# Two-block decoder step: other row ratios around the convolution norm, and means of the raw products one channel tile earlier

## The chip, the cores and the metric

The kernel runs on one core of a Trainium2 chip. The metric is the device time of one execution in microseconds. Three executions of the kernel before gave 1777.66 to 1778.84 us, with a median of 1777.99 us. A fourth one was profiled; the trace that is read here is of that one.

## What is computed

The reference has two blocks in a row on 256 tokens of 1024 channels. In the first, each of two layers normalises the tokens, shifts and scales them by rows that come from a conditioning vector, projects them, runs four branches (retention, short convolution, conformer convolution with a layer norm, attention), and merges them. Layer 0 does so for 256 context tokens too, so it works on 512 columns; layer 1 works on 256. A final norm ends the block. Cut to what matters:

```
for l in range(DEPTH):                                   # first block
    shift, scale, gate = split(silu(c) @ w_mod[l] + b_mod[l])
    h = rmsnorm(x, norm_w[l]) * (1 + scale) + shift
    p = split(h @ w_in[l])
    f = silu(layer_norm(dwconv31(glu(p.cf)) + b)) * silu(p.cf_z)   # "conv" branch
    merged = sum(sigmoid(g[i]) * (branch[i] @ w_branch[i]) for i in range(4))
    x = x + gate * (merged @ w_out[l])
x = rmsnorm(x, final_norm_w)
for i in range(2):                                       # second block
    m = split(silu(c_2) @ ada_w[i] + ada_b[i], 6)
    x = x + m.gt_m * rmsnorm(mixer_i(rmsnorm(x) * (1 + m.sc_m) + m.sh_m))
    x = x + m.gt_f * rmsnorm(conv_ffn(rmsnorm(x) * (1 + m.sc_f) + m.sh_f))
```

## The kernel before

**Products.** The channels lie on the 128 partitions in eight tiles (k = 0 to 7), the tokens on the free axis. Every product of a large weight is made of three: each 128x1024 chunk of a weight comes by DMA into `wr` (SyncE's queue), ScalarE rounds it to `wh` (L166), and VectorE subtracts, `wl` = `wr` - `wh` (L169); data are split into `r` pairs in the same way. TensorE then runs high by high, high by low and low by high (L189). Four `wh`/`wl` pairs exist, so ScalarE can round a chunk only when TensorE has let go of the one four chunks ago. In stages of 512 columns the results go through banks `pm`, of which there are four.

**Work beside the products.** Branch work is written as generators in a queue `hiq` (attention, the convolution's taps, `layer_norm`, `retention`). `pump(us)` (L192), called after each product, runs pieces of them against a credit; `until(st, key)` (L207) runs them to a mark: "att" is the end of attention, "ln" that of the convolution's norm.

**Modulation rows.** Shift, scale and gate of layer 1 and of the second block are matrix-vector products that VectorE makes, one weight row of 128x1024 at a time: a multiplication with a running sum whose full output goes to a scratch tile, so it is called `junk` in the trace (L498). The row is fetched on GpSimd's queue into one of two buffers `ad` (`fetch_row`, L483); the fetch of row n+2 is issued when row n has been used. A `wmodT` row is used twice in layer 0's part (two vectors, `sb_c` and `sb_c_ctx`), each of the 96 `adaT` rows once. There are 152 such instructions. They wait in a second queue `loq`; `pump` takes from it once its count `pumps`, which starts below zero, is above zero: `spare` grows by `ratio * us` and each row costs 1.15 of it (2.3 if used twice). `flush_lo` (L214) issues the rest before a place that needs the results: before layer 0's and layer 1's output product.

**Norms between the stages.** The first product after an output product is begun on raw data ("raw-product step", `start4`, L338): eight channel tiles times four outputs, and the norm's factors are multiplied in afterwards. A callback `mid(k)` is called within tile k: there the squares are summed by TensorE (`means` L549, or `row_sum` L407), `rsqrt` (L429; a ScalarE square root with a table load and a VectorE reciprocal) is taken, and `spread` (L441) copies a column to all 128 columns by a transpose (L443). ScalarE then brings the result out of the bank, and the next `r` pairs (`mod_tile` L558 in layer 1, `maker` L1466 in the second block) need it.

**Order.** A scheduler places each engine's instructions in one fixed list; an engine works its list in order, and what waits holds up what stands behind it.

Of the kernel before, what the change touches and what calls it, by code (L numbers as in the profile page):

```python
# [18 lines left out]
P = 128  # L19
# [85 lines left out]
class Core:  # L105
# [645 lines left out]
    def first_block(self):  # L751
        nc, A, cst = self.nc, self.A, self.cst
        with self.tc.manual_schedule():
            xs, ps, hs = self.start()
        self.last = self.end
        for l in range(2):
            N = 512 if l == 0 else 256
            if l == 1:
                rb = self.T()

                def mid(k):
                    if k == 4:
                        st["pc"] = self.psa()
                        self.means(st["pc"], 0, acc[0].groups(), True, True)
                    if k == 5:
                        st["r"] = self.small(4)
                        self.rsqrt(st["r"], st["pc"][:, 0:4])
                    if k == 7:
                        pb = self.psa()
                        for t in range(4):  # L770
                            self.spread(pb[:, t * P:(t + 1) * P], st["r"][:, t:t + 1])
                        self.act(rb, pb)
                ps, _ = self.start4(lambda k: raws[k], S + 2, mid=mid)
                hs = [(self.R(), self.R()) for _ in range(KT)]
            mod = lambda k, s: self.mod_tile(k, xs[k], rb, self.acol, self.mod[1], hs[k], s)
            norm = lambda p: self.normed(self.T(S), p, rb[:, :S])
            merged = self.mixer(l, hs, N, ps, mod, norm)
            del hs
            acc, st = [Sum(self) for _ in range(1 + l)], {}
            if l == 0:  # L780
                self.src.extend(self.quad(A["win"][1], 32, 36))
                self.flush_lo(lambda: self.done_mods[1])
                a1, sh = self.acol[:, :, 0], self.mod[1][:, 0:8, 0]
            else:
                self.src.extend(self.quad(A["rgi"], 8, 10))
                self.flush_lo(lambda: self.done_mods[2])
                self.ada_columns()
                a1, sh = self.afw, self.ada4[:, 0, 0]
            sh = self.shift_parts(sh, f"sh{l}")
            raws = []  # L790
            first = self.two_tiles(merged, N)
            for n in range(KT):
                ps = first[n] if n < 2 else self.tile_gemm(merged, N)
                for s in range(N // S):
                    c = slice(s * S, (s + 1) * S)
                    x = xs[n][:, c]
                    self.stt(x, ps[:, c], self.gate[l][:, n, s:s + 1], x, ALU.mult, ALU.add)
                q = self.T(N)
                self.act(q, xs[n][:, :N], AF.Square)
                acc[0].push(q)  # L800
                if n == KT - 1 and l == 0:
                    acc[0].push(None)
                if l == 1:
                    q = self.T(S)
                    self.act(q, xs[n][:, :S], AF.Square, scale=self.par("final_norm_w", n))
                    acc[1].push(q)
                raws.append(self.raw_tile(xs[n][:, :S], a1[:, n:n + 1], sh, n))
                self.pump(0.5)
        st = {}

        def mid(k):

            if k == 4:
                rows = self.psa()[0:2, :S]
                parts = [a.groups() for a in acc]
                for m in range(4):
                    self.row_sum(rows, m % 2, 2, [parts[m % 2][m // 2]], 1024, m == 0, m == 3)
                st["sb"] = self.row_copy(rows, 2, S)
            if k == 5:
                pc = self.row_columns(st["sb"], 2, S)  # L820
                r, s, t = [self.cst.tile([P, 2], F32, name="fin" + n) for n in "rst"]
                self.rsqrt(r, pc[:, :, 0])
                self.tt(t, r, r, ALU.mult)
                self.tt(t, t, pc[:, :, 1], ALU.mult)
                self.rsqrt(s, t)
                self.tt(s, s, r, ALU.mult)
                st["s"], st["r"], self.xx = s, r, t
        ps, _ = self.start4(lambda k: raws[k], S + 2, mid=mid)
        return [x[:, :S] for x in xs], ps, st["r"], st["s"]

# [51 lines left out]
    def mixer(self, l, hs, N, first, mod, norm):  # L882
        nc, A = self.nc, self.A
        NS = N // S
        bud = (3.0, 1.0)[l]
        self.pumps, self.spare = -(10, 30)[l], 0.0
        self.ratio = (0.5, 0.6)[l]
        if l:
            self.src.extend(self.mixer_chunks(l))
        self.ahead()  # L890
# [307 lines left out]

        gates(1, br[1], True, False)
        self.until(st, "att")  # L1200
        br[3] = []
        for i in range(4):
            z = silu2(proj())
# [85 lines left out]
            st["ret"] = 1  # L1289

        self.until(st, "ln")
        self.ratio = (0.6, 0.6)[l]
        self.hiq.append(retention())
        br[2] = []
        for i in range(4):
# [11 lines left out]
        return merged  # L1307


    def second_block(self, xs, ps, r, s):  # L1310
        nc, A, cst = self.nc, self.A, self.cst
        self.rgw = [self.load_plain(A["rgw"][g]) for g in range(4)]
        self.rgo = [self.load_plain(q) for q in self.quad(A["rgo"], 0, 2)]
        rb = self.psa()
        for i in range(2):
            self.spread(rb[:, S + i * P:S + (i + 1) * P], s[:, i:i + 1])
        for i in range(2):
            self.spread(rb[:, i * P:(i + 1) * P], r[:, i:i + 1])
        rs, rf = self.T1(), self.T1()
        self.act(rs, rb[:, S:])  # L1320
        self.act(rf, rb[:, :S])
        mk = self.maker(xs, rs, self.afw, self.ada4[:, 0, 0])
        first = lambda c: self.normed(self.T1(), ps[c], rs)

        def finish(k):

            self.stt(xs[k], xs[k], self.par("final_norm_w", k), rf, ALU.mult, ALU.mult)

        for i in range(2):
            nxt = self.quad(A["ffu"][i], 0, NFF)  # L1330
            mk = self.rglru(xs, mk, nxt, first, finish) if i == 0 else self.gla(i, xs, mk, nxt)
            nxt = self.quad(A["gli"], 0, 2) if i == 0 else ()
            mk = self.ffn(i, xs, mk, nxt)
# [505 lines left out]
def build(nc, tc, A):  # L1839
    with ExitStack() as ctx:  # L1840
        k = Core(nc, tc, ctx, A)
        with ExitStack() as c1:
            k.adp = c1.enter_context(tc.tile_pool(name="adp", bufs=2, reuse_waits="tile"))
            k.setup()
            k.t2 = c1.enter_context(tc.tile_pool(name="t2", bufs=58, reuse_waits="tile"))
            fin = k.first_block()
        k.t1 = ctx.enter_context(tc.tile_pool(name="t1", bufs=74, reuse_waits="tile"))
        k.g4 = ctx.enter_context(tc.tile_pool(name="g4", bufs=12, reuse_waits="tile"))
        k.second_block(*fin)

# [53 lines left out]
```

## Time and profile before

| | |
|---|---|
| median of three runs | 1777.99 us |
| the profiled execution | 1775.62 us |
| its span in the trace | 1773.8 us |
| TensorE busy | 1729.2 us, 97% of the span |
| VectorE busy | 1365.3 us, 77% |
| ScalarE busy | 915.8 us, 52% |
| `junk` on VectorE, 128 of one vector | 156.3 us, 51.1 us idle before them |
| clock of TensorE, mean of the span | 0.993 of full |

The page gives busy time and share of each engine first, then the span in 40 slices, the DMA queues, the chain that ended last, and the costliest groups of instructions with the idle time before them and its releaser. The timeline of an engine lists its instructions with start, duration and, in brackets, the idle time before with what ended it. A duration is longer than the distance to the next start where instructions overlap.

### The profile page before, as it was taken

To read this page: it belongs to the slowest core of one execution; us is meant where nothing else is said; L and a number is where in the kernel's file an instruction comes from. 1 tells how busy PE (TensorE), PEld (TensorE's weight loads), DVE (VectorE), ACT (ScalarE), POOL (GpSimd) and SP (SyncE) were. 2 spreads that over 40 slices of the span, in tenths; PEclk is the share of its full clock that TensorE was granted. 3 is DMA by queue.
4 is the path that set the end of the run, shared out by engine and by line. 5 is a ranking of instruction groups with operands and counts; after the bars stand their busy time and mean duration, and the time that the engine had idled before them with its cause. 6 is when DMAs were issued, how large, how long until landed. Compare 5 with 4: busy or idle time off the path is not lost.

```text
span 1773.8 us, 29675 instructions
## 1 busy us (share of the span) xinstructions
PE 1729.2 (97%) x11538; PEld 1552.3 (88%) x11538; DVE 1365.3 (77%) x2501; ACT 915.8 (52%) x1565; POOL 77.3 (4%) x161
## 2 busy tenths in 40 slices
PE   8999999899999999999999999999999999999998
PEld 5787788688978888898998999898999989989998
DVE  4797599976577786697499877779887669788864
ACT  5426642432342333546642554685776565656663
POOL 0000000011011110000000000100000000000000
PEclk9999999999999999999999999999999999999999
DMA  9433234467347674443376466632555633445553
GB/s 346 153 118 109 82 131 143 145 223 248 125 152 244 240 255 154 135 161 120 126 245 235 160 218 196 217 130 90 198 188 165 193 120 109 135 137 182 188 173 114
DMA packets 94302, 301.60 MB, mean 170 GB/s; under 512 B 10049, under 2 KB 11841, under 8 KB 94161
## 3 DMA queue, kind: packets, MB, share of 16 engines
q1 hardware_dynamic: 72096, 225.00, 37.9%
q0 software_dynamic: 19584, 71.31, 12.2%
q10 hardware_dynamic: 2480, 3.39, 0.6%
q8 instruction: 91, 1.49, 0.3%
q14 instruction: 51, 0.41, 0.1%
HBM read 298.61 MB, written 1.05 MB: 169 GB/s over the span
## 4 chain that ended last, share of the span: by engine, by line
PE 70%; issue 17%; DVE 6%; ACT 5%; DMA 1%; POOL 0%; DVEq 0%; POOLq 0%; ACTq 0%
PE pm L189 54%; PE pa L189 13%; ACT t L166 3%; DMA ad<-adaT 1%; DVE wl L169 1%; DVE t L169 1%; DVE t L186 1%; ACT wh L166 1%; PE pa L554 1%; PE pa L1129 1%; PE pa L1721 1%; PE pa L411 1%; DVE x L169 0%; PE pa L606 0%; ACT L166 0%
## 5 line engine op out<-in xcount | busy, mean ns | idle before, releaser
L189 PE MATMUL pm<-r,wh 128*128 128x256 f32 (+2 forms) x5344 | 1211.3, 320 | 16.0 <-ACT r L166 8.5
L189 PEld LDWEIGHTS pm<-r,wh 128*128 128x128 f32 x5344 | 889.7, 191 | 103.9 <-ACT r L166 12.8
L189 PE MATMUL pm<-r,wl 128*128 128x256 f32 (+2 forms) x2672 | 846.4, 319 | 0.5 <-DVE wl L169 0.5
L166 ACT ACTIVATE wh<-wr 128x1024 fp32r<-128x1024 f32 (+1 forms) x408 | 425.8, 1049 | 529.4 <-PE pm L189 395.7
L169 DVE TENSOR_TENSOR wl<-wr,wh 128x1024 fp32r<-128x1024 f32 (+1 forms) x408 | 492.2, 1210 | 174.7 <-ACT wh L166 165.4
L189 PEld LDWEIGHTS pm<-r,wl 128*128 128x128 f32 x2672 | 508.5, 191 | 35.9 <-issue 1.4
L498 DVE SCALAR_TENSOR_TENSOR junk<-ad,sb_c 128x1024 bf16<-128x1024 f32 x128 | 156.3, 1221 | 51.1 <-DMA ad<-adaT 41.0
L189 PE MATMUL pa<-r,wh 128*128 128x256 f32 (+1 forms) x864 | 168.7, 292 | 5.7 <-ACT r L166 5.4
L189 PEld LDWEIGHTS pa<-r,wh 128*128 128x128 f32 x864 | 137.6, 191 | 10.0 <-ACT r L166 6.0
L169 DVE TENSOR_TENSOR t<-t,t 128x256 f32<-128x256 f32 (+2 forms) x278 | 126.4, 470 | 17.5 <-ACT t L166 15.1
L186 DVE SCALAR_TENSOR_TENSOR t<-t,cfw,t 128x482 f32<-128x482 f32 (+29 forms) x240 | 130.7, 601 | 0.0
L189 PE MATMUL pa<-r,wl 128*128 128x256 f32 (+1 forms) x432 | 123.7, 291 | 0.0
L166 ACT ACTIVATE r<-t 128x256 fp32r<-128x256 f32 (+1 forms) x116 | 53.6, 470 | 93.8 <-DVE t L169 55.8
L166 ACT ACTIVATE t<-pm 128x256 f32<-128x256 f32 (+1 forms) x180 | 82.0, 456 | 21.6 <-PE pm L189 21.6
L189 PE MATMUL pa<-t,t 128*64 128x128 f32 (+3 forms) x668 | 89.5, 337 | 0.8 <-ACT t L166 0.8
L189 PEld LDWEIGHTS pa<-r,wl 128*128 128x128 f32 x432 | 82.7, 191 | 1.3
L189 PEld LDWEIGHTS pa<-t,t 128*64 128x64 f32 (+2 forms) x668 | 66.7, 163 | 16.3 <-issue 4.5
L488 POOL DMA_DIRECT2D ad<-adaT x96 | 50.8, 529 | 634.1 <-DVE junk L498 610.4
L189 PE MATMUL pm<-wh,r 128*128 128x256 f32 x384 | 72.7, 288 | 0.0
L166 ACT ACTIVATE t<-t,s 128x512 f32<-128x512 f32 (+2 forms) x104 | 62.7, 635 | 2.9 <-DVE s L181 2.9
L169 DVE TENSOR_TENSOR r<-t,r 128x256 fp32r<-128x256 f32 (+1 forms) x108 | 51.1, 479 | 16.3 <-ACT r L166 16.3
L186 DVE SCALAR_TENSOR_TENSOR t<-t,pm 128x256 f32<-128x256 f32 (+1 forms) x103 | 56.1, 545 | 9.7 <-ACT t L166 7.5
(210 smaller groups left out, 1304.4 us busy)
## 6 DMA issues: line engine op xcount, KB each, us to landing
wr<-win SPq DMA_DIRECT2D x172, 512.0 KB, 4.0
ad<-adaT POOLq DMA_DIRECT2D x96, 512.0 KB, 4.2
wr<-ffu SPq DMA_DIRECT2D x88, 512.0 KB, 3.3
ad<-wmodT POOLq DMA_DIRECT2D x32, 512.0 KB, 3.6
wr<-wbr SPq DMA_DIRECT2D x32, 512.0 KB, 4.3
wr<-ffd SPq DMA_DIRECT2D x32, 512.0 KB, 3.6
wr<-gli SPq DMA_DIRECT2D x24, 512.0 KB, 3.3
t<-wmodN SPq DMA_DIRECT2D x32, 256.0 KB, 5.3
```

The costliest lines, as they stand in the source:

```text
L166: return self.nc.scalar.activation(out=out, in_=in_, func=func, **k)
L169: self.marks.append(self.nc.vector.tensor_tensor(out=out, in0=a, in1=b, op=op).ins)
L186: self.marks.append(self.nc.vector.scalar_tensor_tensor(out=out, in0=a, scalar=s, in1=b, op0=op0, op1=op1).ins)
L189: self.nc.tensor.matmul(out=out, lhsT=lhsT, rhs=rhs, start=start, stop=stop)
L411: self.nc.tensor.matmul(out=rows, lhsT=lhsT, rhs=t, start=(first and i == 0), stop=(last and i == len(tiles) - 1), skip_group_check=True)
L488: self.nc.gpsimd.dma_start(out=raw, in_=self.rows.popleft())
L498: self.nc.vector.scalar_tensor_tensor(out=self.junk, in0=raw, scalar=0.5, in1=v, op0=ALU.mult, op1=ALU.mult, accum_out=o)
L554: self.nc.tensor.matmul(out=bank[:, nt * j + t:nt * j + t + 1], lhsT=q[:, t * P:(t + 1) * P], rhs=self.inv[inv], start=first and m == 0 an ...
L1129: nc.tensor.transpose(pt[:, kk * P:(kk + 1) * P], s, self.ident)
L1721: nc.tensor.matmul(out=o, lhsT=cb[:, 7 - jj:7 - jj + P], rhs=b8(hd_(X, h))[:, :, jj:8], start=(jj == 0 and h % 2 == 0), stop=(jj == 7), sk ...
```

## The change

Three things are changed.

1. Ratios. Layer 1 begins its rows at pump -16 instead of -30, with 0.7 instead of 0.6. From "att" on, while the convolution's norm is made, the ratio is 0.1 in both layers (0.5 and 0.6 before). From "ln" on it is 0.8 (0.6 before).
2. In layer 1's raw-product step the means stand at k = 3 (4 before), the square root at 4 (5), the spread at 5 (7).
3. In the raw-product step that ends the first block, sums and roots stand at 3 and 4 (4 and 5). The two spreads and their copies out of the bank, which stood behind that step in `second_block`, are made in it at k = 6 and go into one tile `rsf`; `second_block` takes its halves `rf` and `rs`. Two pools lose 1 and 2 buffers for it.

```
@@ first_block, layer 1 @@
-                    if k == 4:
+                    if k == 3:
                         st["pc"] = self.psa()
                         self.means(st["pc"], 0, acc[0].groups(), True, True)
-                    if k == 5:
+                    if k == 4:
                         st["r"] = self.small(4)
                         self.rsqrt(st["r"], st["pc"][:, 0:4])
-                    if k == 7:
+                    if k == 5:
                         pb = self.psa()
@@ first_block, last step @@
-            if k == 4:
+            if k == 3:
                 rows = self.psa()[0:2, :S]
...
-            if k == 5:
+            if k == 4:
                 pc = self.row_columns(st["sb"], 2, S)
...
+            if k == 6:
+                rb = self.psa()
+                rows = self.cst.tile([P, 512], F32, name="rsf")
+                for j, c in enumerate((st["s"], st["r"])):
+                    h = slice(j * S, (j + 1) * S)
+                    for i in range(2):
+                        self.spread(rb[:, j * S + i * P:j * S + (i + 1) * P], c[:, i:i + 1])
+                    self.act(rows[:, h], rb[:, h])
+                    st["sr"[j]] = rows[:, h]
@@ mixer @@
-        self.pumps, self.spare = -(10, 30)[l], 0.0
-        self.ratio = (0.5, 0.6)[l]
+        self.pumps, self.spare = -(10, 16)[l], 0.0
+        self.ratio = (0.5, 0.7)[l]
...
         self.until(st, "att")
+        self.ratio = 0.1
...
         self.until(st, "ln")
-        self.ratio = (0.6, 0.6)[l]
+        self.ratio = 0.8
@@ second_block @@
-    def second_block(self, xs, ps, r, s):
+    def second_block(self, xs, ps, rf, rs):
...
-        rb = self.psa()
-        for i in range(2):
-            self.spread(rb[:, S + i * P:S + (i + 1) * P], s[:, i:i + 1])
-        for i in range(2):
-            self.spread(rb[:, i * P:(i + 1) * P], r[:, i:i + 1])
-        rs, rf = self.T1(), self.T1()
-        self.act(rs, rb[:, S:])
-        self.act(rf, rb[:, :S])
```

In the lists below a name ends in the number of its tile. VectorE in layer 0, where the norm of the convolution branch is taken; `t_741`, `t_743`, `t_2246` and `t_2248` are the four tiles of that branch, `s_2852` the root, `pa` its spread. Before:

```order
L169 TENSOR_TENSOR r_2869<-t_2864,r_2868 128x512
L169 TENSOR_TENSOR wl_2947<-wr_2944,wh_2946 128x1024
L498 SCALAR_TENSOR_TENSOR junk,mod_151<-ad_2810,sb_c 128x1024
L498 SCALAR_TENSOR_TENSOR junk,mod_151<-ad_2810,sb_c_ctx 128x1024
L431 RECIPROCAL s_2852<-s_2852 128x4
L169 TENSOR_TENSOR wl_3002<-wr_2999,wh_3001 128x1024
L186 SCALAR_TENSOR_TENSOR t_741<-t_741,prm,pa_2855 128x512
```

and now, the same place:

```order
L169 TENSOR_TENSOR wl_2943<-wr_2940,wh_2942 128x1024
L169 TENSOR_TENSOR t_2790<-t_2790,t_2796 128x512
L169 TENSOR_TENSOR r_2869<-t_2864,r_2868 128x512
L431 RECIPROCAL s_2852<-s_2852 128x4
L186 SCALAR_TENSOR_TENSOR t_741<-t_741,prm,pa_2855 128x512
L186 SCALAR_TENSOR_TENSOR t_743<-t_743,prm,pa_2855 128x512
L186 SCALAR_TENSOR_TENSOR t_2246<-t_2246,prm,pa_2855 128x512
L186 SCALAR_TENSOR_TENSOR t_2248<-t_2248,prm,pa_2855 128x512
L169 TENSOR_TENSOR wl_2994<-wr_2991,wh_2993 128x1024
```

The two rows ahead of the reciprocal are gone, the chunk behind the next one (`wl_2947`, now `wl_2943`) stands before the sum of squares is complete, and the chunk that stood ahead of the four tiles stands behind them.

VectorE in layer 1, at the sum over the four tiles (`t_8810`, now `t_8777`) from which TensorE makes the mean `pa_8847` (now `pa_8814`). Before:

```order
L169 TENSOR_TENSOR t_8810<-t_6305,t_6307 128x256
L169 TENSOR_TENSOR wl_8844<-wr_8841,wh_8843 128x1024
L169 TENSOR_TENSOR t_8810<-t_8810,t_8224 128x256
L498 SCALAR_TENSOR_TENSOR junk,ada<-ad_8770,sb_c_3457 128x1024
L169 TENSOR_TENSOR t_8810<-t_8810,t_8226 128x256
L1221 TENSOR_REDUCE s_8890<-pm_8865 128x2
L181 TENSOR_SCALAR s_8890<-s_8890 128x2
L169 TENSOR_TENSOR t_6305<-t_6305,pa_8847 128x256
```

and now:

```order
L169 TENSOR_TENSOR t_8777<-t_6272,t_6274 128x256
L169 TENSOR_TENSOR wl_8730<-wr_8727,wh_8729 128x1024
L169 TENSOR_TENSOR t_8777<-t_8777,t_8215 128x256
L169 TENSOR_TENSOR t_8777<-t_8777,t_8217 128x256
L169 TENSOR_TENSOR wl_8772<-wr_8769,wh_8771 128x1024
L169 TENSOR_TENSOR t_6272<-t_6272,pa_8814 128x256
```

No row stands within the sum any more, and a weight chunk stands between the sum and the first use of the mean. On TensorE the mean's product moves 46 weight products towards the front.

ScalarE at the end of the first block; `fins` and `finr` are the two roots, `t_11054` and `t_11055` the copies of their spreads, `r_11087` the high part of the second block's first tile (now `r_11086`). Before:

```order
L166 ACTIVATE fins<-fint,eps 128x2
L166 ACTIVATE wh_11072<-wr_11070 128x1024
L166 ACTIVATE wh_11078<-wr_11076 128x1024
L166 ACTIVATE t_11054<-pa_11049 128x256
L166 ACTIVATE t_11055<-pa_11049 128x256
L166 ACTIVATE r_11087<-t_11086,ada 128x256
```

and now:

```order
L166 ACTIVATE fins<-fint,eps 128x2
L166 ACTIVATE rsf<-pa_11007 128x256 x2
L166 ACTIVATE wh_11071<-wr_11069 128x1024
L166 ACTIVATE wh_11077<-wr_11075 128x1024
L166 ACTIVATE r_11086<-t_11085,ada 128x256
```

The copies moved ahead of the two weight chunks; the first `r` stands behind these as before.

## Rows read from the trace of the kernel before

**Rows 1.** The page: busy time by engine, and one kind of DMA.

```profile
PE 1729.2 (97%) x11538; PEld 1552.3 (88%) x11538; DVE 1365.3 (77%) x2501; ACT 915.8 (52%) x1565; POOL 77.3 (4%) x161
...
ad<-adaT POOLq DMA_DIRECT2D x96, 512.0 KB, 4.2
```

**Rows 2.** Windows: length, busy of five engines (instructions), clock, DMA share, GB/s.

```profile
340.00:355.00 15.00, 10.55 (x34) 7.91 (x34) 13.22 (x23) 5.25 (x10) 1.06 (x2) 0.77 0.25 81
970.00:980.00 10.00, 7.90 (x47) 7.18 (x48) 6.71 (x19) 3.16 (x7) 1.06 (x2) 0.83 0.49 157
900.00:950.00 50.00, 50.00 (x374) 47.95 (x373) 48.62 (x93) 20.36 (x30) 3.70 (x7) 1.00 0.68 225
880.00:930.00 50.00, 49.96 (x420) 49.44 (x415) 42.96 (x75) 22.94 (x34) 3.70 (x7) 1.00 0.69 229
540.00:670.00 130.00, 130.00 (x575) 107.70 (x574) 102.09 (x145) 38.89 (x51) 19.57 (x37) 1.00 0.73 248
```

**Rows 3.** Timeline of TensorE, layer 0's norm: start, duration, operation [idle before].

```profile
340.93 0.50 PE L189 MATMUL pm<-r,wh 128*128 128x512 f32 x1 [0.89 <-ACT r L166]
342.00 0.50 PE L189 MATMUL pm<-r,wh 128*128 128x512 f32 x1 [0.58 <-DVE r L169]
...
345.72 1.22 PE L189 MATMUL pm<-r,wh 128*128 128x512 f32 x2 [2.98 <-DVE t L186]
```

**Rows 4.** Timeline of VectorE in the same stretch.

```profile
333.12 0.17 DVE L431 RECIPROCAL s<-s 128x4 f32<-128x4 f32 x1
334.11 1.23 DVE L169 TENSOR_TENSOR wl<-wr,wh 128x1024 fp32r<-128x1024 f32 x1 [0.81 <-ACT wh L166]
335.29 2.73 DVE L186 SCALAR_TENSOR_TENSOR t<-t,prm,pa 128x512 f32<-128x512 f32 x4
...
344.98 0.68 DVE L186 SCALAR_TENSOR_TENSOR t<-t,pm 128x512 f32<-128x512 f32 x1
```

**Rows 5.** Timeline of ScalarE in the same stretch.

```profile
331.27 1.28 ACT L166 ACT_TABLE_LOAD   x1
```

**Rows 6.** Timelines of VectorE, then TensorE, layer 1's norm.

```profile
970.38 1.23 DVE L498 SCALAR_TENSOR_TENSOR junk<-ad,sb_c 128x1024 bf16<-128x1024 f32 x1 [2.36 <-DMA ad<-adaT]
...
971.53 0.42 DVE L169 TENSOR_TENSOR t<-t,t 128x256 f32<-128x256 f32 x1
...
972.10 1.12 PE L189 MATMUL pa<-t,inv 128*128 128x256 f32 x2 [2.58 <-DVE t L169]
```

**Rows 7.** Timelines of ScalarE, then TensorE, at layer 1's start.

```profile
730.80 1.06 ACT L166 ACTIVATE wh<-wr 128x1024 fp32r<-128x1024 f32 x1 [3.08 <-issue]
...
733.54 0.51 ACT L166 ACTIVATE r<-t,mod 128x256 fp32r<-128x256 f32 x1 [0.26 <-DVE t L186]
...
734.11 0.74 PE L189 MATMUL pa<-r,wh 128*128 128x256 f32 x4 [2.12 <-ACT r L166]
```

**Rows 8.** Timelines of ScalarE, VectorE and TensorE at the second block's start.

```profile
1139.83 2.00 ACT L166 ACTIVATE wh<-wr 128x1024 fp32r<-128x1024 f32 x2 [1.77 <-PE pm L189]
...
1143.71 0.51 ACT L166 ACTIVATE r<-t,ada 128x256 fp32r<-128x256 f32 x1 [1.33 <-DVE t L186]
...
1143.20 0.48 DVE L186 SCALAR_TENSOR_TENSOR t<-x,afw,t 128x256 f32<-128x256 f32 x1
...
1144.27 0.91 PE L189 MATMUL pa<-r,wh 128*128 128x256 f32 x5 [3.25 <-ACT r L166]
```

**Rows 9.** Timeline of VectorE: two rows of a stretch in which rows follow closely.

```profile
409.76 1.22 DVE L498 SCALAR_TENSOR_TENSOR junk<-ad,sb_c 128x1024 bf16<-128x1024 f32 x1
...
434.55 1.23 DVE L498 SCALAR_TENSOR_TENSOR junk<-ad,sb_c 128x1024 bf16<-128x1024 f32 x1 [0.17 <-DMA ad<-adaT]
```

**Rows 10.** Groups of instructions from 540 to 670 us, the rows' group.

```profile
L498 DVE SCALAR_TENSOR_TENSOR junk<-ad,sb_c 128x1024 bf16<-128x1024 f32 x37 | 45.2, 1223 | 23.4 <-DMA ad<-adaT 23.1
```

**Rows 11.** Timelines of VectorE, then TensorE: one weight chunk made and first read.

```profile
659.39 1.22 DVE L169 TENSOR_TENSOR wl<-wr,wh 128x1024 fp32r<-128x1024 f32 x1
...
667.61 0.39 PE L189 MATMUL pm<-r,wl 128*128 128x512 f32 x1
```

More of the change, by code (lines that the diff above doesn't have):

```diff
@@ L1844, in build @@
             k.setup()
-            k.t2 = c1.enter_context(tc.tile_pool(name="t2", bufs=58, reuse_waits="tile"))
+            k.t2 = c1.enter_context(tc.tile_pool(name="t2", bufs=57, reuse_waits="tile"))
             fin = k.first_block()
-        k.t1 = ctx.enter_context(tc.tile_pool(name="t1", bufs=74, reuse_waits="tile"))
+        k.t1 = ctx.enter_context(tc.tile_pool(name="t1", bufs=72, reuse_waits="tile"))
         k.g4 = ctx.enter_context(tc.tile_pool(name="g4", bufs=12, reuse_waits="tile"))
```

## The prediction

> **What bounds the kernel now.** I read the busy time by engine first [rows 1]: TensorE is busy for 1729.2 of 1773.8 us, VectorE for 77%, ScalarE for 52%. So only 44 us can be had at all without taking products away, and the change takes none away: it removes no instruction of any size, it moves them. What it can change is where TensorE sits idle, where its clock falls behind such an idle stretch, and whether VectorE or ScalarE comes too late somewhere else. I therefore went through TensorE's timeline for idle times, and then through the timelines of the engines that ended them. Four places touch the change. In layer 0's norm of the convolution branch TensorE waits 0.89, 0.58 and 2.98 us, 4.45 together [rows 3], and the clock in the 15 us around it is 0.77 [rows 2]: up to 0.23 x 15 = 3.45 us of TensorE's time more, part of it within the wait. In layer 1's norm it waits 2.58 us [rows 6] with a clock of 0.83 over 10 us [rows 2], which is 1.7 us. At layer 1's start it waits 2.12 us [rows 7], at the second block's start 3.25 us [rows 8], in both with the clock up. If all four went away it would be 4.45 + 3.45 + 2.58 + 1.7 + 2.12 + 3.25 = 17.6 us, about 1%. That is the ceiling.
>
> **Layer 0's norm: I take nothing.** The change removes five `junk` instructions on VectorE between 320 and 346 us; at 1.14 us from one start to the next this looks like 5.7 us. But it has to be asked what VectorE did instead of waiting. The two that stood ahead of the reciprocal ran while the root was on its way: ScalarE loaded a table for 1.28 us at 331.27 [rows 5], and the reciprocal could not start before 332.8 us in any case (it did at 333.12 [rows 4]). The next `wl` had to wait 0.81 us for its `wh` [rows 4], and a `wh` can be made only when TensorE gives a buffer back. From 334.11 to the instruction at 344.98 that TensorE waits for [rows 3, 4] VectorE's list holds not one row: it is a solid block of tile work and weight chunks. In the new list the chunk of 1.2 us stands behind the four tile operations of 2.73 us instead of ahead of them; the sum up to the last one is the same. The norm's products on TensorE move only 3 and 5 weight products to the front, 0.226 us each (130.00 us / 575 [rows 2]), so 0.7 to 1.1 us, and that is what the four tiles can start earlier by at best, while the other chunks still wait for TensorE's buffers. I take 0, the bounds are 0 and -7.9 us (4.45 + 3.45), and the value lies near 0 because the last row of the chain, at 344.98, stands behind a block without `junk`.
>
> **Layer 1's norm: -4.3 us.** Here the rows do stand in the chain. The sum of the four tiles is complete with the addition at 971.53, and ahead of it lies a row that waited 2.36 us for its DMA [rows 6]. Some ten fewer `junk` stand on VectorE between 900 us and this sum, and VectorE has hardly any free time there (48.62 of 50 us busy from 900 on [rows 2]): 10 x 1.14 + 2.36 = 13.8 us earlier, so about 958 us. TensorE's mean product moves 46 weight products to the front; one takes 0.119 us (49.96 / 420 [rows 2]), so TensorE asks for the sum 5.5 us sooner than at 969.5 (972.10 - 2.58 [rows 6]): at 964 us. The sum is there 6 us before. What is late next is the rest of that norm (row sum, root, spread), which moves 38 to 40 products, 4.6 us; the subtractions now stand behind a weight chunk, so I see only about 1 us of room there. I take the whole 2.58 + 1.7 = 4.3 us; the bounds are 0 and -4.3.
>
> **Layer 1's start: -1.5 us.** The spread moves 24 products of 0.119 us, 2.9 us, to the front. The first `r`, which TensorE waited 2.12 us for [rows 7], also moves ahead of one of the weight chunks on ScalarE. But two `wh` now stand between it and the second `r`; they wait for TensorE's buffers, which come free only as the last products of the step end. So the second `r` is late by a few tenths, and the tile work on VectorE takes some 1.5 us per tile against 12 x 0.119 = 1.43 us on TensorE, which loses about half a microsecond over the tiles. I take 2.1 - 0.6 = 1.5; bounds 0 and -2.1.
>
> **The second block's start: -1.0 us.** The spreads and copies are done early, but they weren't the last thing: the two `wh` from 1139.83 to 1141.8 waited for TensorE [rows 8] and stand ahead of the first `r` in both lists. Behind them VectorE makes two `wl` before its first tile operation at 1143.20 [rows 8]. The high part can come at about 1142 instead of 1143.71, the low part at 1143.2 instead of 1144.2. TensorE needs both within a few products, so it wins the smaller step, 1.0; bounds 0 and -3.25.
>
> **Rows that come later: +1 us.** About 16 fewer rows are done when the merge products behind layer 0's norm are under way, and the ratio of 0.8 then asks for 46 where 34 stood, between 540 us and the weight chunk made at 659.39 [rows 11]. VectorE's own time covers it (102.09 us of 130 busy [rows 2], 12 x 1.14 = 13.7 more). The fetches may not: there are two buffers. Where rows followed each other closely, ten rows started between 409.76 and 434.55 [rows 9], 24.79 / 9 = 2.75 us each, with waits for the DMA in between; and even at the old ratio VectorE stood 23.4 us waiting for fetches before 37 rows [rows 10]. 46 x 2.75 = 126.5 us. The time at hand is 119 us and the lead of that chunk, 667.61 - 659.39 - 1.22 = 7.0 us [rows 11]: 126. So it is just about full, and what goes over makes TensorE wait for `wl`, since the weight chunks stand behind the rows in VectorE's list. Ten more rows also lie in layer 1's attention and five or six in the flush before its output product, where chunks have leads of some 4 us; there I see up to 1 us. I take +1 for both; the bounds are 0 and +10, the latter for (4.2 + 1.22 + 0.5) / 2 = 2.96 us a row (landing time of [rows 1], one use, half a microsecond to issue again): 46 x 2.96 - 126 = 10.
>
> The Trainium skill's page "DMA: Bandwidth & Descriptors" (section "Anatomy of one DMA — SWDGE (gpsimd) path") gives a fit of 2.0 us plus bytes at 436 GB/s for a transfer from GpSimd's queue; for a row of 512 KB I estimate 3.2 us from it. By that two buffers would give a row every 2.5 us and this term would be 0. The trace differs with 4.2 us [rows 1], and the trace decides.
>
> **Sum.** 0 - 4.3 - 1.5 - 1.0 + 1 = -5.8 us. Against the profiled execution's 1775.62 us that is 1769.8; the median of the three runs lies 2.4 us above the profiled one, so I forecast **1772 us** for the median. About 0.2%, 3.6 us, is what a measurement of this kernel can tell from no change.
>
> **Rivals.**
> *Layer 0 gains after all.* If the norm's chain starts a microsecond earlier and TensorE's four banks come free in step with it, the waits of 4.45 us shrink and the clock stays up: 4 to 8 us more, 1764 to 1768. For it: the rows are gone from just this stretch. Against it: the block from 334.11 on is full without them [rows 4]. Chance 0.12.
> *The gain at layer 1's norm only changes its place.* The mean comes in time, but the root or the spread behind it is then waited for, or the first products at the two starts meet the weight chunks that now stand ahead of them. Then half of the 6.8 us of the three places stays: about 1775 to 1777, no change that can be told. For it: the small room of about 1 us, and two `wh` in the way at both starts [rows 7, 8]. Against it: 6 us of room at the sum itself. Chance 0.25.
> *The rows pace VectorE.* This is the slower end. Between 540 and 670 us each row beyond the pace of the fetches makes the weight chunks late, and TensorE stands. It decides at the time per row: at 2.75 us it costs about nothing, each 0.1 us more costs 4.6 us, so at 2.89 us the gain is gone (1778) and at 2.96 the time is 1782. For it: 23.4 us of waits at a lower demand [rows 10]. Against it: the leads of the chunks, and 2.75 us measured with weight fetches running beside. Chance 0.13 for a time of 1778 to 1784.
> My forecast, 1769 to 1775, has the remaining 0.5.
>
> **Range and chances.** 1765 to 1780 us leaves out the upper end of the last rival and the full gain at layer 0, about 0.2 together. Faster by over 0.2% (below 1774.4): the forecast but for its edge, and the first rival, 0.58. Within 0.2%: 0.29. Slower (above 1781.6): the third rival, 0.13, of which the lower part would only just be told.
>
> **What would show it.** In the changed kernel's trace: at layer 0's norm an idle TensorE of 4 to 5 us and half clock as before (else the first step is wrong); in layer 1's norm no wait over 0.5 us before the mean product and a clock of 1.00; 0.3 to 1 us left at layer 1's start, about 2 us at the second block's start; between 540 and 670 us TensorE busy for all but 1 us, and VectorE's idle time before `junk` above 23 us. Waits of TensorE for `wl` in that stretch of more than 4 us in all would make the prediction wrong, as would a new wait in layer 1's attention.

## The result, and the profile after

The changed kernel is slower: 1799.38 us median of four runs (1795.90 to 1800.86) against 1777.83 us; the ratio is 1.0115, 95% interval 1.0102 to 1.0129. The forecast was 1772, the range 1765 to 1780. The profiled execution took 1800.86 us, 25.2 us more than that of before.

The page of the changed kernel shows little of it: the same instructions, TensorE busy for 12.3 us longer [rows 1]. The number of products is the same, so I put that down to the clock, whose mean is 0.987 of full instead of 0.993.

```profile
PE 1741.5 (97%) x11538; PEld 1558.3 (87%) x11538; DVE 1363.2 (76%) x2501; ACT 915.5 (51%) x1565; POOL 77.3 (4%) x161
```

Where the time came from is found by pairing work. TensorE makes the same 9696 weight products in all these kernels, and in the same sequence but for at most 44 that stand a few places off, so the start of the n-th product can be compared from trace to trace. The table gives, for stretches named by the time in the kernel before, how much longer each kernel's profiled execution took than the kernel before; it is worked out from the traces, one for each kernel. The first column and the last one move by a few microseconds with no change in the work (at the very start, and in the second block); only in three_ad does the edit reach into the first.

| us in before | to 42 | to 352 | to 597 | to 620 | to 688 | to 737 | to 967 | to 986 | to 1076 | to 1112 | to 1156 | to 1753 |
|---|---|---|---|---|---|---|---|---|---|---|---|---|
| changed | +1.1 | -0.9 | 0.0 | **+14.1** | **+6.3** | -1.4 | +0.6 | **-4.8** | **+5.0** | **+3.3** | +1.3 | +0.6 |
| rows_only | +0.4 | +0.1 | 0.0 | +10.8 | +3.3 | 0.0 | +0.6 | -4.8 | +4.2 | +2.3 | +2.2 | +3.0 |
| means_only | 0.0 | -0.9 | 0.0 | 0.0 | 0.0 | -1.4 | -0.1 | -0.4 | 0.0 | 0.0 | -0.1 | +1.0 |
| nofetch | +1.5 | +0.2 | 0.0 | 0.0 | 0.0 | -1.4 | +0.6 | -4.8 | -0.1 | +0.4 | +0.4 | +1.2 |
| layer0_old | +1.5 | -1.2 | 0.0 | 0.0 | 0.0 | -1.5 | +0.6 | -4.8 | +3.3 | +0.2 | +1.7 | +3.0 |
| three_ad | +5.7 | -0.1 | 0.0 | +8.2 | 0.0 | -1.4 | +0.6 | -4.8 | +4.4 | +0.3 | +1.5 | +1.5 |
| dose_07 | -0.1 | -0.9 | 0.0 | +10.1 | 0.0 | -1.4 | +5.1 | -4.8 | +3.7 | +3.3 | -0.1 | -0.3 |
| moved_rows | +1.6 | +0.1 | 0.0 | 0.0 | 0.0 | -1.5 | +6.2 | -4.8 | 0.0 | 0.0 | -0.1 | +0.5 |
| moved_rows_start | +2.3 | +0.5 | 0.0 | 0.0 | 0.0 | -1.4 | +3.4 | -4.8 | 0.0 | 0.0 | +0.9 | +0.7 |
| dense_early | +1.9 | +0.3 | +0.2 | +10.3 | +0.4 | 0.0 | +0.1 | -4.0 | 0.0 | 0.0 | +1.8 | +0.7 |
| dense_late | +1.2 | +0.3 | 0.0 | +4.1 | +3.1 | +0.6 | +0.5 | -4.0 | 0.0 | 0.0 | +0.8 | +1.9 |
| best | -0.3 | -0.6 | +0.3 | 0.0 | 0.0 | -1.4 | +0.8 | -4.8 | 0.0 | 0.0 | -0.1 | +0.9 |

In the changed kernel the two layer norms, at 352 and 986 us, and layer 1's start, at 737 us, come out much as forecast. The loss is in two places: 20.4 us between 597 and 688 us, behind layer 0's norm, and 8.3 us between 986 and 1112 us, behind layer 1's.

TensorE's timeline in the first of them (start, duration, operation, idle before with what ended it) shows five new waits between 605 and 635 us, 9.45 us together:

```profile
613.10 0.80 PE L189 MATMUL pm<-r,wl 128*128 128x512 f32 x1 [2.32 <-DVE wl L169]
...
622.10 0.51 PE L189 MATMUL pm<-r,wh 128*128 128x512 f32 x1 [0.83 <-ACT r L166]
...
624.00 0.50 PE L189 MATMUL pm<-r,wh 128*128 128x512 f32 x1 [1.41 <-DVE r L169]
...
628.25 0.80 PE L189 MATMUL pm<-r,wh 128*128 128x512 f32 x1 [3.52 <-ACT r L166]
...
630.42 0.80 PE L189 MATMUL pm<-r,wh 128*128 128x512 f32 x1 [1.37 <-DVE r L169]
```

One is for a weight chunk; four are for `r`, the split results of the retention branch's tiles. Behind them, in the last merges, four more follow, 0.33, 1.63, 1.01 and 0.58 us; the two largest are

```profile
692.63 0.73 PE L189 MATMUL pm<-r,wh 128*128 128x512 f32 x2 [1.63 <-DVE t L186]
...
702.78 0.49 PE L189 MATMUL pm<-r,wh 128*128 128x512 f32 x1 [1.01 <-ACT r L166]
```

The window from 605 to 635 us (length, busy of TensorE, its weight loads, VectorE, ScalarE, GpSimd with their instructions, clock, DMA share, GB/s) shows the clock with it, 0.83; a stretch of the kernel before that holds the same work, second fence, had no idle time and full clock:

```profile
605.00:635.00 30.00, 20.55 (x72) 15.24 (x71) 22.68 (x34) 8.25 (x12) 4.76 (x9) 0.83 0.74 238
```

```profile
603.00:621.00 18.00, 18.00 (x81) 14.91 (x80) 16.21 (x24) 6.20 (x9) 2.65 (x5) 1.00 0.59 202
```

VectorE's timeline of the changed kernel there tells why:

```profile
605.13 1.22 DVE L498 SCALAR_TENSOR_TENSOR junk<-ad,sb_c 128x1024 bf16<-128x1024 f32 x1 [1.15 <-DMA ad<-adaT]
...
610.07 1.22 DVE L498 SCALAR_TENSOR_TENSOR junk<-ad,sb_c 128x1024 bf16<-128x1024 f32 x1 [3.10 <-DMA ad<-adaT]
...
611.83 1.22 DVE L169 TENSOR_TENSOR wl<-wr,wh 128x1024 fp32r<-128x1024 f32 x1
...
618.19 0.68 DVE L186 SCALAR_TENSOR_TENSOR t<-t,pm 128x512 f32<-128x512 f32 x1
619.54 1.23 DVE L498 SCALAR_TENSOR_TENSOR junk<-ad,sb_c 128x1024 bf16<-128x1024 f32 x1 [0.67 <-DMA ad<-adaT]
...
620.69 0.69 DVE L186 SCALAR_TENSOR_TENSOR t<-t,t 128x512 f32<-128x512 f32 x1
622.11 1.23 DVE L498 SCALAR_TENSOR_TENSOR junk<-ad,sb_c 128x1024 bf16<-128x1024 f32 x1 [0.73 <-DMA ad<-adaT]
...
623.26 0.69 DVE L169 TENSOR_TENSOR r<-t,r 128x512 fp32r<-128x512 f32 x1
```

VectorE stands still for 3.10 us ahead of the row at 610.07, waiting for its fetch, and the weight chunk behind it is then 2.32 us late for TensorE. From then on VectorE works through one tile after the other, out of a bank (618.19), times the branch (620.69), split (623.26), and rows that wait for fetches stand between these steps. TensorE takes each such `r` as soon as it is there.

### The profile page after: what moved, and what is told of

The parts are those of the page before. It is cut to its first block, busy times and chain, and to the rows that moved or that the text cites. A ratio compares the mean times of both kernels' runs of the same rounds, so it can differ in the third digit from the quotient of the medians.

```text
span 1799.0 us, 29668 instructions
## 1 busy us (share of the span) xinstructions
PE 1741.5 (97%) x11538; PEld 1558.3 (87%) x11538; DVE 1363.2 (76%) x2501; ACT 915.5 (51%) x1565; POOL 77.3 (4%) x161
## 5 line engine op out<-in xcount | busy, mean ns | idle before, releaser
L166 ACT ACTIVATE t<-pa 128x512 f32<-128x512 f32 (+2 forms) x100 | 44.8, 511 | 32.2 <-PE pa L189 30.4
```

What stands on the lines that cost most here:

```text
L166: return self.nc.scalar.activation(out=out, in_=in_, func=func, **k)
```

## The experiments

The theory from this trace was W: the denser rows behind the norm (0.8 instead of 0.6) wait for their fetches, and VectorE brings everything behind them late. Rivals were M, that the moved means and spreads cost the time, and O, that the rows' own work on VectorE does.

**The two halves alone.** rows_only is the kernel before with

```
-        self.pumps, self.spare = -(10, 30)[l], 0.0
-        self.ratio = (0.5, 0.6)[l]
+        self.pumps, self.spare = -(10, 16)[l], 0.0
+        self.ratio = (0.5, 0.7)[l]
...
         self.until(st, "att")
+        self.ratio = 0.1
...
-        self.ratio = (0.6, 0.6)[l]
+        self.ratio = 0.8
```

> The kernel before with the ratios of the changed kernel and nothing else of it. Theory W (the denser rows behind layer 0's norm wait for their fetches, and VectorE then brings weight chunks and tile results late): the whole loss of 21.6 us is here, so 1797 to 1802 us, with TensorE idle about 9 us between 605 and 635 us. Rival M (the means and spreads that moved cost the time): 1771 to 1778 us.

Measured: 1797.6 us, ratio 1.0114 (1.0090 to 1.0138). means_only is the rest of the change, with the old ratios:

> The kernel before with the earlier means, roots and spreads alone, ratios as before. Theory W: 1.4 us less at layer 1's start, up to 1 us more or less at the second block's start: 1775.5 to 1779 us. Rival M: 1790 us or more.

Measured: 1774.2 us, ratio 0.9983 (0.9972 to 0.9994), a little below what was expected. M falls: the ratios alone make a loss of that size. The two halves don't add up, though: +19.4 and -4.0 us by the medians, +21.6 together. The table puts most of the difference into layer 0, which lost 20.4 us in the changed kernel and 14.1 in rows_only, although the lists of VectorE, ScalarE and GpSimd are the same in both between 360 and 740 us. It stays open, and tells that a stall of this kind can differ by 6 us between two profiles of the same lists.

**The fetches taken away.** nofetch leaves out the fetches of the `adaT` rows from the third on. It is the changed kernel with, in `fetch_row` (in part; the lines that set `nfetch` and `used` are not shown),

```
+        if self.nfetch >= 34 and self.rows and self.rows[0] is not None:
+            self.rows.popleft()
+            self.raws.append(self.used)
+            return
```

> The changed kernel without the fetches of the adaT rows from the third on: VectorE multiplies one row that is already there again and again (so the second block's shifts, scales and gates are not those of the reference). VectorE's list and its work are the same, only the fetches are gone. Theory W: the 47 us that VectorE waited for fetches go, and with them the stalls at 613 to 631, 682 to 705 and 1072 to 1133 us, some 28 us together: 1770 to 1776 us. Rival O (the rows' own 1.14 us on VectorE make it late, the fetches do not matter): 1793 us or more, with the same stalls. Rival in between: the first stall is halved, 1782 to 1790 us.

Measured: 1773.79 us, ratio 0.9976 (0.9967 to 0.9986). All stalls behind both norms are gone, to 0.4 us (table). The two views that decide are the window of the stage, and the group of the rows between 540 and 690 us (count, busy, mean ns, idle before them):

```profile
605.00:635.00 30.00, 30.00 (x134) 24.85 (x133) 26.34 (x40) 11.83 (x16) 0.00 (x0) 1.00 0.33 106
```

```profile
L503 DVE SCALAR_TENSOR_TENSOR junk<-ad,sb_c 128x1024 bf16<-128x1024 f32 x54 | 65.9, 1220 | 2.1 <-DMA ad<-adaT 1.4
```

In the changed kernel the same group, 540 to 700 us, is

```profile
L498 DVE SCALAR_TENSOR_TENSOR junk<-ad,sb_c 128x1024 bf16<-128x1024 f32 x52 | 63.6, 1222 | 38.0 <-DMA ad<-adaT 37.7
```

VectorE is busier in nofetch's window than in the changed kernel's (26.34 against 22.68 us) and TensorE never waits. So it is not the rows' work, O falls: it is the 38 us that VectorE stood in front of them. nofetch also takes load off the memory (DMA share 0.33 instead of 0.74), so weights that land late could be a rival. The waits of the changed kernel from 540 to 700 us speak against it: none is for a weight's DMA. ScalarE, which rounds the chunks, waits for TensorE to give a buffer back (us in total, times, longest):

```profile
ACT wh L166 <- PE pm L189: 43.1, 12, 6.6
```

**Layer 0 as before.** layer0_old keeps the change but for

```
-        self.ratio = 0.1
+        if l:
+            self.ratio = 0.1
...
-        self.ratio = 0.8
+        self.ratio = (0.6, 0.8)[l]
```

> The changed kernel with layer 0's ratios as before (0.5 up to the norm, 0.6 behind it); layer 1 starts its rows at pump -16 with 0.7, has 0.1 in the norm and 0.8 behind it. Theory W: no loss in layer 0, the 4.8 us at layer 1's norm and the 1.4 us at its start stay, up to 3 us are lost in its attention and its last merges, up to 1 us at the second block's start: 1772 to 1777 us. Rival O or M: over 1778 us, since the same number of rows has to go somewhere.

Measured: 1777.08 us, ratio 0.9986 (0.9972 to 0.9999), just above what W said and below what O or M said: the 20 us are gone, the 4.8 us at layer 1's norm stay, but 3.3 us are lost again behind it, where the ratio is still 0.8.

**Is it the number of buffers?** three_ad has three `ad` buffers (in part; a second place that takes an `ad` buffer is changed likewise, and a pool of 57 loses two):

```
-            raw = self.adp.tile([P, 1024], F32, tag="ad", name=self.nm("ad"))
+            raw = self.adp.tile([P, 1024], F32, tag="ad", bufs=3, name=self.nm("ad"))
...
-        for _ in range(2 - len(self.raws)):
+        for _ in range(3 - len(self.raws)):
```

> The changed kernel with three buffers for fetched rows instead of two, three fetches under way (a pool of 57 loses two buffers for the room). Theory W, part one (it is the landing time over two buffers that limits the rows): (4.3 + 0.3 + 1.2) / 3 = 1.9 us a row are possible, 2.6 are asked for, so the stalls of layer 0 behind the norm (20.3 us) go and most of the 8 us in layer 1's last merges: 1773 to 1781 us. Rival H (the fetches share what the memory gives with the weights, and land later when three are under way): landing over 6 us, still some 3 us a row, 1792 to 1800 us.

Measured: 1789.33 us, ratio 1.0058 (1.0041 to 1.0075), between the two. The wait before the rows falls by half, 545 to 700 us:

```profile
L498 DVE SCALAR_TENSOR_TENSOR junk<-ad,sb_c 128x1024 bf16<-128x1024 f32 x53 | 64.7, 1221 | 18.2 <-DMA ad<-adaT 17.9
```

But the fetches land later with three under way: 5.1 us median against 4.1 in the changed kernel's same stretch. Both theories hold a part. By the table the third buffer takes away the 6.3 us of the last merges and 5.9 of the 14.1 ahead of them; against rows_only it is 3.3 and 2.6, so the size is uncertain. It leaves a single large wait:

```profile
629.20 1.52 PE L189 MATMUL pm<-r,wh 128*128 128x512 f32 x2 [4.55 <-ACT r L166]
```

The time also holds 5.7 us at the very start (table), far ahead of the stalls. The third buffer lets the first row's fetch out at 1.70 us (GpSimd's timeline), where the kernel before issues it at 58.81, and ScalarE then waits 2.82 us for a tile of the input, 0.83 in the kernel before. That this fetch is the cause is likely, not shown.

```profile
1.70 0.71 POOL L488 DMA_DIRECT2D ad<-wmodT  x1
```

**Fewer of them.** dose_07 takes 0.7 instead of 0.8 behind layer 0's norm, and lets layer 1 begin earlier:

```
-        self.pumps, self.spare = -(10, 16)[l], 0.0
-        self.ratio = (0.5, 0.7)[l]
+        self.pumps, self.spare = -(10, 6)[l], 0.0
+        self.ratio = (0.5, 0.9)[l]
...
-        self.ratio = 0.8
+        self.ratio = (0.7, 0.8)[l]
```

> The changed kernel with 0.7 instead of 0.8 behind layer 0's norm: 41 rows instead of 46 in the 126 us at hand. Layer 1 starts its rows at pump -6 with 0.9, so that no more rows than in the changed kernel are left for its last merges. Theory W: 41 x 3.06 = 125.5 us just fit, so the 20.3 us in layer 0 fall to 0 to 5: 1779 to 1786 us, with the 6 to 8 us in layer 1's last merges still there. A theory by which any denser rows hurt in proportion: 16 us of the 20 stay, 1793 us.

Measured: 1789.98 us, ratio 1.0064 (1.0048 to 1.0081). W as I had sized it misses: the last merges of layer 0 are free again, but 10.1 us are still lost at the same place as before,

```profile
612.52 0.50 PE L189 MATMUL pm<-r,wl 128*128 128x512 f32 x1 [2.27 <-DVE wl L169]
...
624.05 1.52 PE L189 MATMUL pm<-r,wh 128*128 128x512 f32 x2 [3.53 <-ACT r L166]
```

and the 23 rows in layer 1's attention cost 5 us. The balance over the whole stretch up to 660 us was the wrong one. In VectorE's list 18 rows stand between the chunk at 541 us and the tiles at 608 us in the kernel before, 25 in the changed kernel, 23 in dose_07, 27 in three_ad (and 27 in nofetch, where nothing waits). If this is the date that counts, the dose had hardly fallen there.

**Where it falls due.** That gave theory L: VectorE falls behind during the gates and products of the convolution branch, unseen, since weight chunks are made well ahead; and it pays in the four tiles that follow, where TensorE, VectorE, ScalarE and VectorE hand a tile on with no lead. dense_early and dense_late are the kernel before with 0.8 only ahead of these tiles, or only from them on:

```
-        self.ratio = (0.6, 0.6)[l]
+        self.ratio = (0.8, 0.6)[l]
...
         self.until(st, "ret")
+        self.ratio = 0.6
```

```
         self.until(st, "ret")
+        self.ratio = (0.8, 0.6)[l]
```

> The kernel before with 0.8 instead of 0.6 behind layer 0's norm, but only until the retention's result is there (the gates and products of the convolution branch); from then on 0.6 again. Theory L (VectorE falls behind while the rows are dense, unseen behind the lead of the weight chunks, and pays at the next stage, where each of four tiles goes from TensorE to VectorE, ScalarE, VectorE and back without lead): a stall of 8 to 14 us appears at 610 to 632 us although no denser rows stand in that stage itself: 1786 to 1792 us. Rival S (only rows that stand within that stage's tile chain cost): 1775 to 1780 us.

> The kernel before with 0.8 instead of 0.6 only from the retention's result on, that is in the four tiles of the retention branch and in the last merge of layer 0. Theory L: VectorE enters the tile chain in time; a row or two more in it costs 0 to 4 us there, and what falls behind in the last merge is paid at the output product, up to 6 us: 1778 to 1787 us. Rival S: the stall of 14 us at 610 to 632 us is there: 1790 us or more.

Measured: dense_early 1787.06 us, ratio 1.0042 (1.0028 to 1.0056); dense_late 1780.82 us, ratio 1.0016 (1.0007 to 1.0026). TensorE's timelines, dense_early first:

```profile
615.09 0.50 PE L189 MATMUL pm<-r,wl 128*128 128x512 f32 x1 [1.95 <-DVE wl L169]
...
627.64 1.52 PE L189 MATMUL pm<-r,wh 128*128 128x512 f32 x2 [3.54 <-ACT r L166]
```

```profile
620.83 0.51 PE L189 MATMUL pm<-r,wh 128*128 128x512 f32 x1 [1.68 <-ACT r L166]
...
692.46 0.49 PE L189 MATMUL pm<-r,wh 128*128 128x512 f32 x1 [1.14 <-ACT r L166]
```

Rows that stand ahead of the tiles make the stall in the tiles, 10.3 us; denser rows within the tiles and behind cost 4.1 and 3.1. L holds, S falls. It can also be read as VectorE's lateness: the 89th weight chunk, just ahead of these tiles, is made 7.0 us later against TensorE's progress than in the kernel before in the changed kernel, 8.4 in three_ad, 9.7 in dose_07, 7.7 in dense_early, 1.1 in dense_late, and 2.3 us earlier in nofetch (worked out by pairing chunks and products). The stalls in the tiles are 14.1, 8.2, 10.1, 10.3, 4.1 and 0.0 us: a late VectorE goes with a stall, but the lateness does not give its size.

**Where the rows could go instead.** moved_rows keeps layer 0 as before and puts 23 rows into layer 1's attention (start at -6 with 0.9; 0.1 in the norm, 0.6 behind it). moved_rows_start is the same without the earlier sums and spreads in the first block's last step.

> Layer 0 as before (0.5, then 0.6); layer 1 starts its rows at pump -6 with 0.9, has 0.1 in its norm and 0.6 behind it, so four rows are left for its merges; means and spreads as in the changed kernel. W: 4.8 us gained at layer 1's norm, 1.4 at its start, up to 1 us lost in its attention, no loss in its merges, between +1 and -1 at the second block's start: 1770 to 1774 us. If the attention can't take 23 rows: over 1776.

> The same rows as in moved_rows, and of the means and spreads only those of layer 1's start; the last step of the first block and the second block's start as before. It tells what the spreads inside the last step are worth: by the traces so far they take 0.8 us of TensorE's time that lay in idle time before and win 0.85 us of waiting, and the clock falls behind them in some runs, so this kernel should take the same time as moved_rows or up to 2 us less: 1769 to 1774 us.

Measured: 1777.89 us, ratio 0.9995 (0.9982 to 1.0009), and 1777.06 us, 0.9992 (0.9983 to 1.0002): no change to be told, and both above what was expected. The merges of layer 1 are free with four rows left, but the attention, where I had allowed 1 us, takes 6.2 and 3.4 us. Two of the waits in moved_rows, TensorE's timeline:

```profile
766.07 0.50 PE L189 MATMUL pm<-r,wl 128*128 128x512 f32 x1 [0.73 <-DVE wl L169]
...
792.32 0.48 PE L189 MATMUL pm<-r,wh 128*128 128x256 f32 x2 [1.54 <-DVE t L169]
```

Between the two kernels nothing can be told at the second block's start.

**A version from it.** best keeps the earlier means and spreads and the 0.1 in layer 1's norm, and puts rows where there was room:

```
-        self.pumps, self.spare = -(10, 16)[l], 0.0
+        self.pumps, self.spare = -(10, 20)[l], 0.0
...
-        self.ratio = 0.1
+        self.ratio = (0.6, 0.1)[l]
...
-        self.ratio = 0.8
+        self.ratio = (0.6, 0.6)[l]
```

> A version meant to keep the gains without the losses: means and spreads as in the changed kernel; layer 0 with 0.5, then 0.6 from the end of attention on (eight rows more in the stretch ahead of its norm, nothing denser behind it); layer 1 begins at pump -20 with 0.7 (seven rows in its attention), has 0.1 in its norm and 0.6 behind it. Theory W: layer 1's norm wins 4.8 us, its start 1.4, its attention loses about 0.7, the rest is even: 1771 to 1774.5 us. If the rows ahead of layer 0's norm are not free: up to 1780 us.

Measured: 1773.73 us, ratio 0.9966 (0.9953 to 0.9978), faster than both kernels. It can't be told from means_only (1774.20 us, 0.9972 to 0.9994), which moves no row. Eight rows more than in the kernel before up to 540 us (one of them ahead of 346 us, seven between there and 540) cost nothing that the table shows (-0.6 and +0.3 us), and the wait at layer 0's norm is as long as ever:

```profile
345.66 1.22 PE L189 MATMUL pm<-r,wh 128*128 128x512 f32 x2 [3.16 <-DVE t L186]
```

## Why the prediction was wrong, point by point

**Layer 0's norm, 0 us: right.** The waits are 0.90, 0.57 and 2.66 us, 4.13 against 4.45 [rows 3], and means_only, with all the rows in place, has the same -0.9 us up to 352 us. Between 320 and 346 us five rows stand in the kernel before and in means_only, none in the changed kernel, six in best (two of them within the block behind 334 us), and the three waits make 4.45, 4.10, 4.13 and 4.64 us. So the five rows don't set this wait; that the block does is argued from VectorE's list.

**Layer 1's norm, -4.3 us: right in size (-4.8), only half right in cause.** The mean product stands without a wait now, and so does the row sum behind it; the clock is full there (second fence, the window):

```profile
983.16 0.59 PE L189 MATMUL pa<-t,inv 128*128 128x256 f32 x2
...
989.43 0.59 PE L411 MATMUL pa<-t,inv 128*1 128x256 f32 x2
```

```profile
980.00:990.00 10.00, 10.00 (x68) 8.83 (x66) 5.13 (x13) 3.22 (x6) 0.00 (x0) 1.00 0.32 107
```

But dense_early and dense_late win 4.0 us here with ten rows standing in the norm as before. VectorE's and TensorE's timelines of dense_early:

```profile
981.21 1.21 DVE L498 SCALAR_TENSOR_TENSOR junk<-ad,sb_c 128x1024 bf16<-128x1024 f32 x1
982.35 0.42 DVE L169 TENSOR_TENSOR t<-t,t 128x256 f32<-128x256 f32 x1
```

```profile
982.91 0.67 PE L189 MATMUL pa<-t,inv 128*128 128x256 f32 x2
```

The row ahead of the sum's last addition is there, but has not waited: what is missing is the 2.36 us of [rows 6]. GpSimd's timeline shows why the kernel before had it, and dense_early, second fence, has not:

```profile
966.05 1.06 POOL L488 DMA_DIRECT2D ad<-adaT  x2 [9.31 <-DVE junk L498]
```

```profile
976.73 0.53 POOL L488 DMA_DIRECT2D ad<-adaT  x1 [6.73 <-DVE junk L498]
```

In the kernel before the fetch was issued 2.9 us after the row that freed its buffer, together with the next one; in dense_early 0.3 us after it. So by these traces one late fetch made 4.0 of the 4.8 us, the ten rows the rest. I had the 2.36 us in the sum, but as one part of 13.8 us of room: that the size came out is partly luck. Why the fetch was released late is open. The rival by which this gain only changes its place is refuted: in nofetch the 4.8 us stay, and no more than 0.4 us is lost in any stretch from there to 1156 us.

**Layer 1's start, -1.5 us: right, -1.4.** It is -1.4 or -1.5 in every kernel with the earlier means, and 0.0 or +0.6 in the three without. A wait of 0.71 us for the second `r` stays (0.27 for the first), as forecast.

**The second block's start, -1.0 us: wrong, about 0 in means_only, +1.3 in the changed kernel.** The waits did shrink, from 3.25 us [rows 8] to 1.70 + 0.70 in means_only and 1.80 + 0.71 in the changed kernel. The failing step is that the spreads were priced at nothing. In the kernel before they ran while TensorE was waiting anyway; now, in means_only's timeline, they stand among the products,

```profile
1135.70 0.40 PE L443 MATMUL pa<-ident,fins 128*128 128x128 f32 x2
1136.58 0.43 PE L443 MATMUL pa<-ident,finr 128*128 128x128 f32 x2
```

and the products behind them come 0.8 us later, which is the 0.85 us that were won. What the changed kernel loses beyond that I put down to the clock: it is 0.83 from 1165 to 1175 us, where [rows 8] lie in a stretch of full clock (second fence, the kernel before).

```profile
1165.00:1175.00 10.00, 7.49 (x48) 7.07 (x47) 9.05 (x20) 3.68 (x6) 0.73 (x2) 0.83 1.02 416
```

```profile
1140.00:1150.00 10.00, 6.75 (x50) 5.99 (x50) 8.81 (x19) 4.41 (x8) 4.92 (x8) 1.00 0.78 301
```

**Rows that come later, +1 us: wrong, +20.4 in layer 0 and +8.3 in layer 1's merges.** This is the term that decided, and three things were wrong in it.

First, the price of a row. I took 2.75 us from ten rows in a stretch where VectorE had little else to do [rows 9] (it was busy for 15.73 of 24.79 us, the rows counted in). The 52 rows between 542.18 and 698.37 us of the changed kernel follow at 156.19 / 51 = 3.06 us (3.00 up to 605 us, ahead of the first stall). The fetches are no slower: 4.1 us median to landing, against 4.2 on the page before [rows 1]. It is the round of two buffers, (4.3 mean landing + 0.3 to issue again + 1.2 use) / 2 = 2.9, and on top of it, I take it, a landed row waits until VectorE is through with a chunk or a tile. My upper bound, 2.96, was the better value, and was still exceeded. The fit of the Trainium skill's page "DMA: Bandwidth & Descriptors" (section "Anatomy of one DMA — SWDGE (gpsimd) path"), 3.2 us for such a transfer by my estimate, would have hidden the term altogether. No trace here bears the 3.2 us out beside the weights: the median of the `adaT` rows is 3.8 to 4.5 us in every kernel with two buffers.

Second, the date. I balanced 46 rows against the weight chunk at 659 us and its lead of 7 us. But results fall due earlier, in the four tiles at 610 to 632 us, and there no chunk's lead helps, since TensorE waits for `r`. 25 rows of 3.06 us are 76 us, and 66 are at hand up to that point. The two signs that I had named for a wrong prediction looked at the wrong operand and the wrong place: TensorE waited 2.32 us for `wl`, not over 4, and layer 1's attention had no new wait; but TensorE, which was to be busy for all but 1 us from 540 to 670 us, was idle for 9.45.

Third, the clock. 9.45 us of idle time cost 14.1 us, and the rest is lower clock around the waits (0.83 over 30 us, which is 5.1 us, part of it within the waits). I had counted it for every wait that might go, and for none that might come.

The rival "the rows pace VectorE" had the mechanism and the stretch right, and its deciding point, 2.89 us a row, was passed. That the weight chunks would be late was right for one wait of five. It got a chance of 0.13 and ended at 1784, by the same bound of 2.96 us and without the clock; the range left its upper end out on top. Its evidence, 23.4 us of waits at the lower ratio [rows 10], was weightier than the 2.75 us that spoke against it.

In layer 1 the 8.3 us come with two groups of waits: 0.65, 0.48 and 1.57 us at its retention tiles, and 0.64 and 1.71 us with the last rows ahead of the output product. I had allowed 1 us for the latter and nothing for the former. In nofetch none of them is there.

## What to carry to other kernels

Work that is fetched through a small ring of buffers has a least distance of (landing + issue + use) / buffers, 2.9 us here, and on a busy engine more than that, 3.06 us here; ask for less than this rate, since the engine that consumes it stands still in front of it with everything that is queued behind. Lateness is not paid where it arises but at the first stage that hands tiles on without lead, so the balance is to be made up to that stage, and priced with the clock that may fall behind the wait. An idle stretch that is shortened may have held other work for nothing; price that work when it is moved out.

## What was not expected of the hardware

Three fetches under way from GpSimd's queue beside the weights' stream landed after 5.1 us (median) instead of 4.1 with two. The weights' own chunks landed later too (`win`: 6.1 us instead of 4.6). So the third buffer brought one row in 2.74 us instead of one in 3.08, both from 540 to 632 us.

The clock does not follow the length of a wait alone. The same wait of 3.25 us at the second block's start left the clock at full in the kernel before ([rows 8], and 1.00 in its window from 1140 to 1150 us above); in dense_early, with the same products around it, the window there shows 0.66:

```profile
1150.00:1160.00 10.00, 6.75 (x36) 6.51 (x35) 9.55 (x20) 3.64 (x8) 4.92 (x8) 0.66 0.84 323
```

In the table dense_early takes 1.8 us more in this stretch with no change in the work, about as much as the smaller terms of the prediction.
